# Two halves of rows in turn in the delta rule's state update, and one two-bank tile for both score maps of a head

## The chip, the cores and the metric

The kernel runs on one core of a Trainium2 chip. The metric is the device time of one execution in microseconds. The engines are named as the profile names them: PE (TensorE products; PEld its weight loads), DVE (VectorE), ACT (ScalarE), POOL, and SP, whose queue issues nearly all loads. All of them run their own instructions in order and wait for each other through semaphores.

## The reference, cut to what matters

Two layers of a block that mixes tokens in three branches, for 256 context tokens and 256 tokens of x, 1024 features, float32. The two parts that the change touches are the differential attention and the gated delta rule:

```python
def diff_softmax_combine(q, k, v, lam):                      # q, k: [b, 4 heads, 2 maps, n, 64]
    s = jnp.einsum('bhmqd,bhmkd->bhmqk', q, k) * B_HEAD_DIM ** -0.5
    p = jax.nn.softmax(s, axis=-1)
    a = p[:, :, 0] - lam * p[:, :, 1]
    return jnp.einsum('bhqk,bhkd->bhqd', a, v)

# gated delta rule, chunks of 64 tokens, forward and backward
def step(state, blk):
    u_c, w_c, qd_c, in_c, kt_c, gt_c = blk
    v_new = u_c - jnp.einsum('bhcd,bhde->bhce', w_c, state)
    o_c = jnp.einsum('bhcd,bhde->bhce', qd_c, state) + jnp.einsum('bhij,bhje->bhie', in_c, v_new)
    state = state * gt_c[..., None, None] + jnp.einsum('bhcd,bhce->bhde', kt_c, v_new)
    return state, o_c
```

Around them stand the modulation, a root-mean-square normalisation, the projections, a spatial gating branch, the gated sum of the branches and a feed-forward block with a convolution. In the second layer (the last) only the 256 tokens of x are wanted at the end.

## The kernel before, in words

**Products.** Each large product is made of float32r parts: weights come by DMA as float32 (`wr`), ACT rounds them to `wh`, DVE takes the rest `wl`, and three products per 128 rows (`mm3`) add up in a PSUM bank. The small products of attention and of the delta rule are plain float32; the trace shows each of them as two weight loads and two passes.

**PSUM.** There are eight banks of 512 float32 per partition, in four rotating groups (`BANKS`): "p" two, "g" three, "a" two, "b" one. A new tile of a group waits until an old one is released, that is, until all that reads it is done. "a" serves in turn the factor `pb` of the normalisation (`norm_end`), two column tiles of the key projections (`gdn_begin`), in layer two every second convolution tile (`gdn_conv`), the modulation products `pmod` of the mixer (`mod`), the transposed queries and keys `pqkT` (`attn_project`), and the score maps `psc` (`attn_core`).

**Order.** The framework lays out each engine's order when the kernel is built: of the instructions that its own estimate of time has as ready, the one earliest in the program goes first. Blocks in `high_priority(offset=AHEAD)` count as earlier; among them are the whole delta-rule preparation, `gdn_solve` and `gdn_scan`, between whose steps the products of `attn_project` (`ptm`), of the spatial gating (`pu`) and of `gdn_z` (`pj`) are set. In the attention the products of the branches (`pg`, `pbr`) fill in.

**Delta rule.** `gdn_scan` runs eight steps in each layer (`gdn_step`). A step works on one tile of 128 tokens: two chunks of 64, one going forward and one backward, one on partitions 0 to 63 and one on 64 to 127 (`R[0]`, `R[1]`). For the four heads it makes `pkS` (keys times state), `rhs`, `pV` (times the inverse), `vn`, where an output is wanted `pq` and `pgo`, and last `pS`, the update of the state `S` (in the trace `gS`): for each direction one bank, four products with 64 rows, then four updates on DVE. In all other products of a step the two halves alternate.

**Attention.** `attn_core` goes over tiles of 128 queries and four heads: in layer one four tiles (two with 256 keys, two with 512), in layer two two tiles with 512 keys, 24 heads in all. For each head: two score maps (`psc`, 64 rows each, map 0 on partitions 0 to 63 and map 1 on 64 to 127) in a bank of "a" each, the maximum of each on DVE, one small operation that makes the bias, two exponentials with sums on ACT, the weight `w`, the combined map, its transposition (`paT`), and the product with the values (`po`).

The steps of the change are in `bank` (line 201), `attn_core` (807 to 834) and `gdn_step` (1270 to 1280).

Of the kernel before, what the change touches and what calls it, by code (L numbers as in the profile page):

```python
# [20 lines left out]
D = 1024  # L21
# [136 lines left out]
def steps(it, *counts):  # L158
    """goes along with `it` by each of `counts` at a time."""
    for n in counts:  # L160
        for _ in range(n):
            next(it, None)
        yield
# [9 lines left out]
class _Kernel:  # L173
    def __init__(self, tc, a, out, es, dbg):
        self._gt = (None, None)
        self.tc, self.nc, self.a, self.out, self.dbg = tc, tc.nc, a, out, dbg or {}
        pool = lambda n, b, **k: es.enter_context(tc.tile_pool(name=n, bufs=b, **k))
        self.cp = pool("cp", 1)
        self.wp = pool("wp", 2)
        self.hp = pool("hp", 1)  # L180
        self.sp = pool("sp", 1)
        self.tp = pool("tp", 3)
        self.dp = pool("dp", 1, space=bass.MemoryType.DRAM)
        self.ps = pool("ps", 1, space=PSUM)
# [14 lines left out]
    BANKS = {"p": 2, "g": 3, "a": 2, "b": 1}  # L199

    def bank(self, tag, name):
        return self.ps.tile([128, 512], F32, tag=tag, name=name, bufs=self.BANKS[tag])

# [37 lines left out]
    def rsqrt(self, out, src, scale, bias, chain):  # L241
        """out = 1 / sqrt(src * scale + bias) for small tiles; bias a float, a tile of out's shape
        or, for a bare src, None."""
        nc = self.nc
        shape = list(out.shape)
        v, t = (self.cp.tile(shape, F32, tag="rsq" + n + chain, name="rsq" + n, bufs=1) for n in "vt")
        if bias is None:
            v = src
        elif isinstance(bias, float):
            self.ts(v, src, scale, bias, ALU.mult, ALU.add)  # L250
        else:
            self.stt(v, src, scale, bias, ALU.mult, ALU.add)
        self.ts(out.bitcast(I32), v.bitcast(I32), -0.5, float(0x5F3759DF), ALU.mult, ALU.add)
        self.mul(t, out, out)
        self.mul(t, t, v)
        self.stt(t, t, -10 / 3, t, ALU.add, ALU.mult)
        self.stt(out, t, 5.0, out, ALU.add, ALU.mult)
        self.mul(t, out, out)
        self.stt(t, t, -0.5 * 0.375 ** 3, v, ALU.mult, ALU.mult)
        self.stt(out, t, 1.5 * 0.375, out, ALU.add, ALU.mult)  # L260
# [10 lines left out]
    def wblock(self, src, n, step):  # L271
        """the two float32r parts of a block of weights [128, n], in pieces of `step` columns."""
        hi, lo = [], []
        r = self.wload(src, n)
        for s in range(0, n, step):
            m = min(step, n - s)
            h = self.wp.tile([128, m], F32R, tag="wh", name="wh", bufs=4)
            o = self.wp.tile([128, m], F32R, tag="wl", name="wl", bufs=4)
            self.split(h, o, r[:, s:s + m])
            hi.append(h)  # L280
            lo.append(o)
        return hi, lo
# [6 lines left out]
    def proj_fm(self, src, kt, xh, xl, c0, ps):  # L289
        """ps[:, :NT-c0] = W^T x for one column tile of W laid out [128, kt*128]."""  # L290
        wh, wl = self.wblock(src, kt * 128, 512)
        for k in range(kt):
            i, s = k // 4, slice(k % 4 * 128, k % 4 * 128 + 128)
            self.mm3(ps[:, :NT - c0], wh[i][:, s], wl[i][:, s], xh[:, k, c0:], xl[:, k, c0:], k == 0, k == kt - 1)

    def first_load(self, srcs, i, j):
        """half i of the rows of column tiles j and j + 1, to be split by first_w."""
        r = self.wp.tile([128, 2, 512], F32, tag="wr", name="wr2", bufs=3)
        for n in range(2):
            self.nc.sync.dma_start(out=r[:, n], in_=srcs[j + n][:, 4 * i:4 * i + 4].rearrange("p k m -> p (k m)"))  # L300
        self.ahead[i, j] = r
# [13 lines left out]
    def proj_first(self, srcs, xh, xl, c0, pss):  # L315
        """as proj_fm for several column tiles at once; goes along with h as its parts appear."""
# [79 lines left out]
    def load_rest(self):  # L396
        """the constants and parameters that the first products do without."""
# [33 lines left out]
    def mod_load(self, l, g, h, where):  # L431
        """half of the columns of group g, [128, 8, 256], in a slot or in tiles of a part of its size."""
        src = self.a["wmod"][l, g, h]
        if isinstance(where, int):
            r = self.slot(where, "wm", [128, 8, 256])
            self.nc.sync.dma_start(out=r, in_=src)
            return [r[:, k] for k in range(8)]
        r = []
        n = 8 // len(where)
        for i, tag in enumerate(where):  # L440
            t = self.tp.tile([128, n, 256], F32, tag=tag, name="wm2", bufs={"p4": 2, "tg": 4, "go": 4, "ta": 3}.get(tag, 1))
            self.nc.sync.dma_start(out=t, in_=src[:, n * i:n * i + n])
            r += [t[:, k] for k in range(n)]
        return r
# [4 lines left out]
    def mod_product(self, pm, r):  # L449
        """pm[32q + (ctx, x)] = silu(cond) @ w_mod over the features of k = q, q + 4."""  # L450
# [4 lines left out]
    def mod_finish(self, l, pm, j, n):  # L455
        """modv[l][:, j:j+n], features on partitions, [ctx, x]."""
# [9 lines left out]
    def mod(self, l, groups, places, tag="a"):  # L466
        """modv[l] for groups of 4 column tiles, silu(cond) @ w_mod + b_mod; yields after each half of the columns,
        which go through the next of `places` if they aren't there, and after each group."""
# [19 lines left out]
    def norm_begin(self, l, n, xf, c0, slots=(), mods=None):  # L488
        """modulate(rms_norm(x)) split into two float32r parts; x and h are feature-major. `mods` yields when the next
        half of the features has its modulation."""  # L490
# [18 lines left out]
    def norm_add(self, N, k):  # L509
        """column tile k of x: its squares, and x times its gain."""  # L510
# [11 lines left out]
    def norm_end(self, N, fill=iter(())):  # L522
        """`fill` goes along, while the tensor engine would wait."""
# [180 lines left out]
    def proj_tm(self, g, c0, use, ahead=False):  # L704
        """token-major projection onto 256 columns; use(t0, psum) for each pair of tiles of 128 tokens."""
# [22 lines left out]
    def flush(self):  # L728
        """what was put off until after the next products."""
# [77 lines left out]
    def attn_core(self):  # L807
# [5 lines left out]
        for t in range(c0 // 128, 4):  # L813
# [5 lines left out]
            for h in range(4):  # L819
# [4 lines left out]
                pss = []  # L824
                for m in range(2):
                    p = self.bank("a", "psc")
                    self.mm(p[:, :nk], self.aq[64 * m:64 * m + 64, h, 128 * t:128 * t + 128],
                            self.ak[64 * m:64 * m + 64, h, 0:nk])
                    nc.vector.tensor_reduce(out=mx[:, m:m + 1], in_=p[:, :nk], axis=AX.X, op=ALU.max)
                    pss.append(p)  # L830
                self.stt(mx, mx, -1.0, qs, ALU.mult, ALU.mult)
                for m in range(2):
                    self.act(pr[:, m, :nk], pss[m][:, :nk], AF.Exp, scale=qs[:, m:m + 1], bias=mx[:, m:m + 1],
# [37 lines left out]
    def to_tiles(self, dst, src, c0, f):  # L871
        """columns in sequence order -> columns of tiles, each two chunks: 0 and 3, then 1 and 2."""
# [14 lines left out]
    def gdn_conv(self, j, dst, cc, ssp, p=None):  # L887
        """one column tile of the projections through the convolution and silu; sums of squares per token."""
# [24 lines left out]
    def gdn_rsqrt(self, name, ssp, t0):  # L913
        """1 / length and squared length of each head of each token, [128 tokens, tile, head], from sums on 32 partitions
        per tile."""
# [42 lines left out]
    def gdn_beta(self, g):  # L958
        """beta and a projections."""
# [18 lines left out]
    def gdn_keys(self, g):  # L978
        """keys with tokens on partitions, A = strictly lower part of k k^T, decayed and scaled by beta, and the
        decay of queries and keys."""  # L980
# [63 lines left out]
    def gdn_gates(self, pbt, rk, vk):  # L1044
        """decay and write-strength columns, [128 tokens, tile, type, head]. The keys go without their 1 / length:
        with D = diag(1 / length), I + diag(beta) D M D is similar to I + diag(beta) D^2 M by D, so that beta
        takes 1 / length^2 and what goes into and comes out of the inverse the rest."""
# [98 lines left out]
    def gdn_solve(self, g):  # L1146
        """U = transpose of the inverse of I + A (forward) or inverse of I + B (backward), from 32 x 32 blocks."""
# [73 lines left out]
    def gdn_step(self, q, U, S, t, y, first, out_s, o, P):  # L1221
# [48 lines left out]
        for a in range(2):  # L1270
            d = dirs[a]
            pS = self.bank("g", "pS")
            for h in range(4):
                self.mm(pS[:, 128 * h:128 * h + 128], ktok[R[a], t, h, :], vn[R[a], 1, h, :])
            if first:
                self.act(S[:, d].rearrange("p h e -> p (h e)"), pS, AF.Copy)
            else:
                for h in range(4):
                    self.stt(S[:, d, h], S[:, d, h], q["gts"][:, a, t, 4 * y + h:4 * y + h + 1],
                             pS[:, 128 * h:128 * h + 128], ALU.mult, ALU.add)  # L1280
# [102 lines left out]
```

## Time and profile before

| | |
|---|---|
| median of 3 runs | 1662.61 us (1662.46 to 1664.08) |
| profiled execution, span of its instructions (no other time is given for it) | 1662.0 us |
| PE busy | 1623.0 us, 98% |
| DVE busy | 1084.7 us, 65% |
| ACT busy | 760.9 us, 46% |
| loads | 212 MB read, 130 GB/s over the span |

"Busy" is the time in which at least one instruction of the engine is under way. PE's instructions overlap, so a busy PE can still be slow; the distance from one pass's start to the next tells its pace. Times in the rows are microseconds from the start of the span, durations of single instructions are in ns where a row says "mean" and in us elsewhere.

### The profile page before, as it was taken

To read this page: it belongs to the slowest core of one execution; us is meant where nothing else is said; L and a number is where in the kernel's file an instruction comes from. 1 tells how busy PE (TensorE), PEld (TensorE's weight loads), DVE (VectorE), ACT (ScalarE), POOL (GpSimd) and SP (SyncE) were. 2 spreads that over 40 slices of the span, in tenths; PEclk is the share of its full clock that TensorE was granted. 3 is DMA by queue.
4 is the path that set the end of the run, shared out by engine and by line. 5 is a ranking of instruction groups with operands and counts; after the bars stand their busy time and mean duration, and the time that the engine had idled before them with its cause. 6 is when DMAs were issued, how large, how long until landed. Compare 5 with 4: busy or idle time off the path is not lost.

```text
span 1662.0 us, 28498 instructions
## 1 busy us (share of the span) xinstructions
PE 1623.0 (98%) x11278; PEld 1355.4 (82%) x11278; DVE 1084.7 (65%) x2557; ACT 760.9 (46%) x1445; POOL 6.6 (0%) x16
## 2 busy tenths in 40 slices
PE   5999999999999999999999999999999999999999
PEld 3777887876788887778888887778878799999999
DVE  5658678666744456756446655658678775788685
ACT  3553622256532333534234442653722764566564
POOL 0000000000000000000000000000000000000000
PEclk9999899999999999999999999999999999999999
DMA  8553111421233444533333335441114356755665
GB/s 327 202 192 118 40 39 52 140 89 39 74 92 102 145 147 155 213 127 93 92 107 101 97 120 169 164 154 52 40 52 140 92 153 224 226 155 174 190 185 153
DMA packets 61254, 217.24 MB, mean 131 GB/s; under 512 B 7104, under 2 KB 13248, under 8 KB 55360
## 3 DMA queue, kind: packets, MB, share of 16 engines
q1 hardware_dynamic: 59248, 207.65, 39.3%
q10 hardware_dynamic: 1872, 7.77, 1.3%
q8 instruction: 88, 1.44, 0.4%
q14 instruction: 46, 0.38, 0.1%
HBM read 212.25 MB, written 3.15 MB: 130 GB/s over the span
## 4 chain that ended last, share of the span: by engine, by line
PE 88%; DVE 5%; ACT 2%; DMA 2%; issue 1%; SPq 0%; ACTq 0%; DVEq 0%
PE pup L239 22%; PE pg L239 11%; PE pdn L239 11%; PE pqkv L239 7%; PE ptm L239 7%; PE pbr L239 6%; PE pwo L239 3%; PE pmod L239 3%; PE pu L239 2%; PE psc L239 2%; PE pS L239 2%; PE pj L239 1%; ACT U L236 1%; PE pkS L239 1%; PE po L239 1%; PE pV L239 1%
## 5 line engine op out<-in xcount | busy, mean ns | idle before, releaser
L236 ACT ACTIVATE wh<-wr 128x512 fp32r<-128x512 f32 (+1 forms) x594 | 367.6, 622 | 441.8 <-PE pdn L239 108.5
L218 DVE TENSOR_TENSOR wl<-wr,wh 128x512 fp32r<-128x512 f32 (+1 forms) x592 | 400.1, 680 | 236.1 <-ACT wh L236 233.3
L239 PE MATMUL pup<-hh,wh 128*128 128x512 f32 (+1 forms) x704 | 237.9, 338 | 1.0 <-ACT hh L236 0.9
L239 PE MATMUL pup<-hh,wl 128*128 128x512 f32 (+1 forms) x704 | 236.8, 337 | 0.0
L239 PE MATMUL pup<-hl,wh 128*128 128x512 f32 (+1 forms) x704 | 236.2, 336 | 0.0
L233 DVE SCALAR_TENSOR_TENSOR fcv<-pup,par,fcv 128x510 f32<-128x510 f32 (+1 forms) x176 | 107.3, 611 | 81.4 <-ACT fcv L236 81.1
L239 PEld LDWEIGHTS pup<-hh,wh 128*128 128x128 f32 x704 | 133.6, 190 | 17.6 <-ACT fcv L236 2.5
L239 PEld LDWEIGHTS pup<-hl,wh 128*128 128x128 f32 x704 | 133.5, 190 | 14.0 <-DVE hl L233 0.2
L239 PEld LDWEIGHTS pup<-hh,wl 128*128 128x128 f32 x704 | 133.7, 190 | 13.6
L239 PE MATMUL ptm<-wh,hh 128*128 128x256 f32 x448 | 132.1, 295 | 0.0
L239 PE MATMUL ptm<-wh,hl 128*128 128x256 f32 x448 | 131.4, 294 | 0.0
L239 PE MATMUL pg<-hh,wl 128*128 128x512 f32 (+1 forms) x384 | 130.8, 341 | 0.0
L239 PE MATMUL pg<-hh,wh 128*128 128x512 f32 (+1 forms) x384 | 130.7, 340 | 0.1
L239 PE MATMUL ptm<-wl,hh 128*128 128x256 f32 x448 | 130.6, 292 | 0.0
L239 PE MATMUL pg<-hl,wh 128*128 128x512 f32 (+1 forms) x384 | 129.9, 338 | 0.0
L239 PE MATMUL pdn<-fh,wh 128*128 128x512 f32 (+1 forms) x352 | 118.5, 337 | 0.0
L239 PE MATMUL pdn<-fh,wl 128*128 128x512 f32 (+1 forms) x352 | 118.3, 336 | 0.0
L239 PE MATMUL pdn<-fl,wh 128*128 128x512 f32 (+1 forms) x352 | 118.0, 336 | 0.0
L236 ACT ACTIVATE fcv<-pup,par 128x512 f32<-128x512 f32 (+1 forms) x88 | 51.1, 581 | 91.1 <-PE pup L239 91.1
L239 PEld LDWEIGHTS ptm<-wh,hh 128*128 128x128 f32 x448 | 88.1, 197 | 4.7 <-issue 4.2
L239 PEld LDWEIGHTS ptm<-wh,hl 128*128 128x128 f32 x448 | 88.2, 197 | 3.3 <-issue 2.9
L239 PEld LDWEIGHTS ptm<-wl,hh 128*128 128x128 f32 x448 | 87.9, 196 | 2.8 <-issue 2.2
(326 smaller groups left out, 3121.9 us busy)
## 6 DMA issues: line engine op xcount, KB each, us to landing
wr<-in_wup_dram SPq DMA_DIRECT2D x80, 512.0 KB, 3.7
wm<-in_wmod_dram SPq DMA_DIRECT2D x39, 1024.0 KB, 7.6
wr<-in_wfm_dram SPq DMA_DIRECT2D x78, 512.0 KB, 3.6
wr<-in_wtm_dram SPq DMA_DIRECT2D x32, 512.0 KB, 3.7
wr<-in_wdn_dram SPq DMA_DIRECT2D x32, 512.0 KB, 3.6
wr<-in_wbr_dram SPq DMA_DIRECT2D x24, 512.0 KB, 3.6
wr<-in_wo_dram SPq DMA_DIRECT2D x16, 512.0 KB, 4.3
wm<-in_wmod_dram SPq DMA_DIRECT2D x14, 512.0 KB, 4.2
```

The lines of the kernel that those rows point to most:

```text
L218: self.nc.vector.tensor_tensor(out=out, in0=a, in1=b, op=op)
L233: self.nc.vector.scalar_tensor_tensor(out=out, in0=a, scalar=s, in1=b, op0=op0, op1=op1)
L236: self.nc.scalar.activation(out, a, f, bias=bias, scale=scale, **k)
L239: self.nc.tensor.matmul(out, lhsT, rhs, start=start, stop=stop, **k)
```

## The change

The state update's two banks are taken together, and its products and updates go by head, the two halves of rows in turn. The score maps of a head lie in one tile of two banks, `[128, 2, 512]`, with one buffer; one reduction takes both maxima. Since group "a" is now this one tile, everything else that used it takes the halves of such a tile in turn, and a new one is made when both are given out.

```diff
-    BANKS = {"p": 2, "g": 3, "a": 2, "b": 1}
+    BANKS = {"p": 2, "g": 3, "b": 1}
 
     def bank(self, tag, name):
+        if tag == "a":
+            if not self.half:
+                pair = self.pair(name)
+                self.half = [pair[:, 1], pair[:, 0]]
+            return self.half.pop()
         return self.ps.tile([128, 512], F32, tag=tag, name=name, bufs=self.BANKS[tag])
+
+    def pair(self, name):
+
+        self.half = []
+        return self.ps.tile([128, 2, 512], F32, tag="a", name=name, bufs=1)
...
-                pss = []
+                pss = self.pair("psc")
                 for m in range(2):
-                    p = self.bank("a", "psc")
-                    self.mm(p[:, :nk], self.aq[64 * m:64 * m + 64, h, 128 * t:128 * t + 128],
+                    self.mm(pss[:, m, :nk], self.aq[64 * m:64 * m + 64, h, 128 * t:128 * t + 128],
                             self.ak[64 * m:64 * m + 64, h, 0:nk])
-                    nc.vector.tensor_reduce(out=mx[:, m:m + 1], in_=p[:, :nk], axis=AX.X, op=ALU.max)
-                    pss.append(p)
+                nc.vector.tensor_reduce(out=mx, in_=pss[:, :, :nk], axis=AX.X, op=ALU.max)
                 self.stt(mx, mx, -1.0, qs, ALU.mult, ALU.mult)
                 for m in range(2):
-                    self.act(pr[:, m, :nk], pss[m][:, :nk], AF.Exp, scale=qs[:, m:m + 1], bias=mx[:, m:m + 1],
+                    self.act(pr[:, m, :nk], pss[:, m, :nk], AF.Exp, scale=qs[:, m:m + 1], bias=mx[:, m:m + 1],
                              accum_out=sm[:, m:m + 1])
...
-        for a in range(2):
-            d = dirs[a]
-            pS = self.bank("g", "pS")
-            for h in range(4):
-                self.mm(pS[:, 128 * h:128 * h + 128], ktok[R[a], t, h, :], vn[R[a], 1, h, :])
-            if first:
-                self.act(S[:, d].rearrange("p h e -> p (h e)"), pS, AF.Copy)
-            else:
-                for h in range(4):
-                    self.stt(S[:, d, h], S[:, d, h], q["gts"][:, a, t, 4 * y + h:4 * y + h + 1],
-                             pS[:, 128 * h:128 * h + 128], ALU.mult, ALU.add)
+        pSs = [self.bank("g", "pS") for _ in range(2)]
+        for h in range(4):
+            for a in range(2):
+                self.mm(pSs[a][:, 128 * h:128 * h + 128], ktok[R[a], t, h, :], vn[R[a], 1, h, :])
+        if first:
+            for a in range(2):
+                self.act(S[:, dirs[a]].rearrange("p h e -> p (h e)"), pSs[a], AF.Copy)
+            return
+        for h in range(4):
+            for a in range(2):
+                self.stt(S[:, dirs[a], h], S[:, dirs[a], h], q["gts"][:, a, t, 4 * y + h:4 * y + h + 1],
+                         pSs[a][:, 128 * h:128 * h + 128], ALU.mult, ALU.add)
```

## Rows read from the trace of the kernel before

**Rows 1.** The page: busy time by engine, and the chain that ended last.
```profile
PE 1623.0 (98%) x11278; PEld 1355.4 (82%) x11278; DVE 1084.7 (65%) x2557; ACT 760.9 (46%) x1445; POOL 6.6 (0%) x16
...
PE 88%; DVE 5%; ACT 2%; DMA 2%; issue 1%; SPq 0%; ACTq 0%; DVEq 0%
```
**Rows 2.** Busy times by stretch (us, instructions), clock, DMA: scan and attention, each layer.
```profile
205.00:304.00 99.00, 99.00 (x936) 77.84 (x933) 75.70 (x248) 23.30 (x39) 0.00 (x0) 1.00 0.16 49
341.00:440.00 99.00, 97.41 (x454) 67.25 (x453) 66.21 (x213) 62.08 (x164) 0.00 (x0) 1.00 0.20 59
1201.00:1272.00 71.00, 70.11 (x649) 53.94 (x648) 54.93 (x167) 16.05 (x27) 0.00 (x0) 1.00 0.23 68
1300.00:1340.00 40.00, 38.90 (x227) 27.95 (x227) 28.57 (x82) 27.82 (x72) 0.00 (x0) 1.00 0.27 80
```
**Rows 3.** The chain in order of time (start, us, piece), in the second scan.
```profile
1247.75 1.64 PE pS L239 x16
```
**Rows 4.** Groups by shape on PE: count, busy us, mean ns, idle before.
```profile
L239 PE MATMUL psc<-akT,qhT 64*128 64x512 f32 x64 | 28.5, 641 | 0.2 <-ACT pr L236 0.2
L239 PE MATMUL pS<-vn,ktok 64*128 64x128 f32 x256 | 27.4, 285 | 0.6 <-DVE vn L218 0.6
L239 PE MATMUL psc<-akT,qhT 64*128 64x256 f32 x32 | 8.9, 428 | 0.0
```
**Rows 5.** Time line of PE (start, us to the last end, instruction): one step.
```profile
233.82 1.09 PE L239 MATMUL pgo<-vn,inT 64*64 64x128 f32 x16
234.84 1.71 PE L239 MATMUL pS<-vn,ktok 64*128 64x128 f32 x16
236.48 0.38 PE L239 MATMUL ptm<-wh,hl 128*128 128x256 f32 x1
```
**Rows 6.** Time line of weight loads in that step, two short windows.
```profile
235.17 0.30 PEld L239 LDWEIGHTS pS<-vn,ktok 64*128 64x128 f32 x2
...
235.40 0.41 PEld L239 LDWEIGHTS pS<-vn,ktok 64*128 64x128 f32 x6
```
**Rows 7.** Time line of DVE, the same step's updates of the state.
```profile
236.30 2.15 DVE L233 SCALAR_TENSOR_TENSOR gS<-gS,g_gts,pS 128x128 f32<-128x128 f32 x8
```
**Rows 8.** Time line of PE: score products of four heads.
```profile
367.26 0.70 PE L239 MATMUL psc<-akT,qhT 64*128 64x256 f32 x4
...
371.67 0.70 PE L239 MATMUL psc<-akT,qhT 64*128 64x256 f32 x2
...
410.81 1.12 PE L239 MATMUL psc<-akT,qhT 64*128 64x512 f32 x2
...
1309.08 1.55 PE L239 MATMUL psc<-akT,qhT 64*128 64x512 f32 x4
```
**Rows 9.** Groups by shape from 300 to 1340: maxima on DVE, exponentials on ACT.
```profile
L829 DVE TENSOR_REDUCE mx<-psc 128x1 f32<-128x512 f32 x32 | 21.8, 686 | 5.1 <-PE psc L239 4.7
L829 DVE TENSOR_REDUCE mx<-psc 128x1 f32<-128x256 f32 x16 | 6.5, 419 | 3.4 <-PE psc L239 2.9
...
L236 ACT ACTIVATE pr<-psc,mx,qscale 128x512 f32<-128x512 f32 x32 | 24.6, 774 | 2.6 <-DVE mx L233 2.5
L236 ACT ACTIVATION_READ_ACCUMULATOR pr<-psc,mx,qscale 128x1 f32 x47 | 9.3, 199 | 0.0
```
**Rows 10.** Waits (us in total, times, longest), 341 to 440 and 1300 to 1340.
```profile
PEld psc L239 <- ACT pr L236: 2.3, 9, 0.4
...
PEld psc L239 <- ACT pr L236: 0.9, 2, 0.5
```
**Rows 11.** Time line of DVE, normalisation at the start of layer two.
```profile
1042.03 1.69 DVE L233 SCALAR_TENSOR_TENSOR hl<-xn,modv,hh 128x256 fp32r<-128x256 f32 x4
...
1049.36 1.28 DVE L218 TENSOR_TENSOR xn<-xn,pb 128x512 f32<-128x512 f32 x2
```
**Rows 12.** The chain in order of time, the key projections of layer two.
```profile
1042.45 22.22 PE pqkv L239 x96
```
**Rows 13.** Time line of PE, modulation products in layer one.
```profile
81.99 2.78 PE L239 MATMUL pmod<-wm,scond 128*32 128x256 f32 x42
```

More of the change, by code (lines that the diff above doesn't have):

```diff
@@ L174, in __init__ @@
     def __init__(self, tc, a, out, es, dbg):
-        self._gt = (None, None)
+        self._gt, self.half = (None, None), []
         self.tc, self.nc, self.a, self.out, self.dbg = tc, tc.nc, a, out, dbg or {}
```

## The prediction, before the changed kernel was run

> **What bounds the kernel now.** I read the page first. PE is busy 98% of the span, and the chain of work that ended last is 88% PE [rows 1]; the other engines are busy two thirds of the time or less. So an edit is worth what it takes out of PE's own stream, as long as other work stands ready for PE in that stage. That is the next thing to look for, in the busy times by stage [rows 2]: in both delta-rule scans (205 to 304 and 1201 to 1272) and both attention stages (341 to 440 and 1300 to 1340) PE is busy 97% or more, while DVE has 67 to 77% and ACT 23 to 70%. The reader should see that no second engine is near its limit there, and that PE is fed by other products between the steps. The chain of waits agrees: fifteen of the sixteen state updates of the scans stand on it as whole pieces of 1.6 to 1.7 us, of which one row is shown [rows 3]. The two things that the change touches are therefore on the path: the state update's products (pS) keep PE 27.4 us in all, the score products (psc) 28.5 + 8.9 = 37.4 us [rows 4]. "Busy" is not speed, though; the last thing to read is at what pace these passes go, and that is where both edits act.
>
> **The change, part by part.**
>
> *1. State update, products.* A step has 8 products, each of two passes, 16 in all. Half of them use array rows 0 to 63, half rows 64 to 127. Now all 8 passes of the first half go ahead of the second. The time line of one step shows pS starting at 234.84 and the next product at 236.48, so 1.64 us; just ahead of it pgo, with the same 16 passes and operands of the same length but its two halves in turn, takes 1.02 us to pS's start [rows 5]. The weight loads of pS show why. Early in the step two loads take 0.30 us: one load lasts 0.19, so they start 0.11 apart, one after the other. In the middle, where the first half's end meets the second half's beginning, six loads take 0.41 us: 0.22 for five starts [rows 6]. There the two halves run side by side, two passes per 0.11 us. With the halves in turn the whole step should run like its middle: 8 pairs at 0.11 us plus one pass of 0.285 [rows 4] is 1.17 us in place of 1.71 [rows 5], 0.54 less. Sixteen steps: 8.6 us. The best end is pgo's own length, 1.09: 0.62 x 16 = 9.9 us. The worst end is no gain, if the full-width loads can't keep up over a whole step (a rival below). I take 8.5 us, since the nearest row is this very tile's middle.
>
> [...]
>
> *2. State update, on DVE.* The 8 updates of a step take 2.15 us, 0.27 each [rows 7], and keep their number and size. The next step's first product needs head 0 in both directions: now after the 5th update, then after the 2nd, 0.8 us sooner; its last product needs the 8th either way. PE has ptm and pu products to do meanwhile [rows 2], so I cost this at nothing. Both PSUM banks must be free before the first pair, where now the second is needed half a step later; its former reader (tq or vn) is over before pgo starts in most steps, so nothing again. If that cover is gone, either is worth at most 0.8 us in 14 steps, 11 us, to one side or the other.
>
> *3. Scores, products.* A head's two maps are two products of two passes, again on the two row halves. The rows show them in three states [rows 8]: of 256 columns, four passes issued together take 0.70 us, as long as two alone (0.70); of 512 columns, one map alone takes 1.12 us, and two issued near each other 1.55. Now the second map has its own bank and its own wait, so that many heads come in two pieces or half overlapped. With one tile both wait for the same thing and start together: 16 heads x 1.12 + 8 heads x 0.70 = 23.5 us in place of 37.4 [rows 4]. That is 13.9 us less at best.
>
> *4. Scores, the wait.* What pays for it: the tile has one buffer, so the first product of the next head waits until both exponentials have read it. Now it waits for one. The second exponential and its sum take 0.774 + 0.199 = 0.97 us [rows 9]. PE runs in order; behind the waiting product stand paT and po of the head before, and the filling products of the branches; who waits for those is ACT and DVE with the weights' splits. Nothing to the full 0.97 us in 24 heads (23.3 us) can become idle PE. Today PE's wait for that release is 2.3 + 0.9 us over the two stages [rows 10], with other products laid in between, and more of them are to be had in both stages. I take 0.3 us a head, 7 us, nearer to the row than to the bound. So parts 3 and 4 together: 7 us less; ends 13.9 less and 9.4 more.
>
> *5. Scores, the maximum.* Two reductions become one. From 419 ns at 256 columns and 686 at 512 [rows 9], 267 ns per 256 columns, one of 1024 should take 1.22 us and one of 512 0.69: DVE loses 0.15 us x 24 = 3.7 us of work, where it is not the bound [rows 2]. But the step from the second product's end to the exponentials grows by 0.53 us (512 columns). The attention stages have the later branch's products to fill PE, so nothing; uncovered it would be 0.53 x 16 = 8.6 us.
>
> *6. The same two banks elsewhere.* All users of tag "a" (modulation products, the normalisation's pb, key projections, pqkT) now get halves of one tile, and a new pair must wait for both halves of the old one. In the second layer the key projections 2 and 3 wait for pb, which is read until 1050.64, while products run from 1042.45 [rows 11, 12]. Today three of four column tiles can go with the features as they appear; then two, 6 products per feature tile at 22.22 / 96 = 0.23 us, 1.4 us, against 1.28 / 2 + 1.69 / 2 = 1.49 us of DVE per feature tile. So PE is a little short: about 0.1 us x 6, plus a start, 1 us. In the first layer the modulation products that fill a hole at 82 to 88 (42 of them in 2.78 us) [rows 13] belong to two groups; the second must then wait until the first has been read, and 32 products, 2.1 us, go to another place, where PE may have a hole too. I take 2 us for the whole part; the ends are 0 and 8, for the later convolutions of layer two, which take halves in turn.
>
> **Sum.** -8.5 - 7 + 2 = -13.5 us on the profiled execution's span of 1662.0 gives 1648.5. The median of the runs is 1662.61, 0.6 above that span, so I predict 1649 us. Its own range, from the sizes of parts 1, 4 and 6, is 1643 to 1655.
>
> **The rivals.**
>
> A. *The scores give nothing back.* PE starts the pair together but stands for it as long as it saves, because the order of PE's instructions is laid out at build and the exponentials come later than it assumes. For it: in the second layer's attention heads follow each other by the chain product, maximum, exponential. Against: small waits today [rows 10]. -8.5 + 2 gives 1656.
>
> B. *Weight loads take turns.* Part 1 gives nothing, the scores as forecast: -7 + 2, 1657.6. For it: two single loads are 0.11 us apart. Against: the middle of the step [rows 6]. [...]
>
> C. *Slower: the pair's release starves PE.* Place: the 24 heads. Price: 0.97 us of wait and up to 0.53 us of longer maximum, 1.5 us a head, 36 us if all of it lies open, against 13.9 + 8.5 us saved and 2 us lost at the other users of the banks. It decides when more than 20.4 / 36 = 57% is open; at 80% it is 28.8 - 20.4 = +8.4, 1671 us. For it: one buffer where there were two, and an engine that runs in order. Against: both stages have products of three branches to put between.
>
> D. *All of it pays.* -9.9 - 13.9, nothing lost: 1639 us.
>
> E. *It does not do what it says*: neither pair overlaps further, since what sets the pace is issue, not rows: 1662 us.
>
> **How the numbers follow.** Forecast 0.50, A 0.18, B 0.06, C 0.12, D 0.07, E 0.07. What a measurement of this kernel can tell from no change is about 0.2%, 3.3 us: faster means under 1659.3. The forecast, D, A and most of B are faster: 0.78. E and the edges of A and B are the same: 0.11. C is slower: 0.11. The range that leaves out no more than 2 in 10 takes in D, the forecast, A and B: 1639 to 1662.
>
> **What would show it.** Part 1: pS from its start to the next product at 1.1 us a step in place of 1.64, and 18 to 19 us in all in place of 27.4; at 1.6 B is right. Part 3: psc at 1.12 and 0.70 us a head, 24 us in all. Part 4: PE's wait for the release by the exponentials; above 20 us, C. Part 6: PE idle or slow near 85 and between 1042 and 1054. If PE's busy groups shrink as said and the span does not, the prediction is wrong in its premise that PE sets the time of these stages.

## The result, and the profile after

The changed kernel takes 1688.45 us (median of 4 runs, 1685.03 to 1689.43), the kernel before beside it 1663.34 (1662.46 to 1665.03): a ratio of 1.0138, 95% interval 1.0126 to 1.0150, so 23 us slower where 14 us faster was predicted. (The two medians lie 25.1 us apart, just outside that interval; the text goes by the ratios.) All ratios here and below are of fast executions; one of e12's ten (3121.33 us) was slow and counts in its median alone. The profiled execution took 1689.18 us, its span 1687.4.

The page of the changed kernel: busy time of PE, the clock that PE was granted in 40 slices, and the chain that ended last.
```profile
PE 1630.1 (97%) x11278; PEld 1352.2 (80%) x11278; DVE 1086.3 (64%) x2533; ACT 766.5 (45%) x1449; POOL 6.6 (0%) x16
...
PEclk9989999999999999999999999899999999999999
...
PE 82%; DVE 8%; ACT 5%; issue 2%; DMA 1%; SPq 0%; ACTq 0%; DVEq 0%
```
Against [rows 1] the reader sees the same 11278 PE instructions, 7 us more busy time, and a chain that is PE for 82% in place of 88%, with 6 more points for DVE and ACT together (13 for 7). Nothing in these lines says where. Three places do.

**What the change was meant to do, it did.** The time line of PE, one step of the changed kernel's first scan (start, us to the last end, instruction), answers [rows 5]; the next two fences are the weight loads of one step [rows 6], of the kernel before (the step of [rows 5]) and of the changed one, the last fence its score products [rows 8].
```profile
220.75 0.93 PE L249 MATMUL pgo<-vn,inT 64*64 64x128 f32 x14
221.61 1.16 PE L249 MATMUL pS<-vn,ktok 64*128 64x128 f32 x16
222.70 0.39 PE L249 MATMUL ptm<-wh,hh 128*128 128x256 f32 x1
```
```profile
234.84 1.52 PEld L239 LDWEIGHTS pS<-vn,ktok 64*128 64x128 f32 x16 [0.17 <-issue]
```
```profile
221.61 0.97 PEld L249 LDWEIGHTS pS<-vn,ktok 64*128 64x128 f32 x16 [0.17 <-issue]
```
```profile
381.62 0.70 PE L249 MATMUL psc<-akT,qhT 64*128 64x256 f32 x4
...
434.32 1.13 PE L249 MATMUL psc<-akT,qhT 64*128 64x512 f32 x4
```
pS runs 1.09 us from its start to the next product where it took 1.64, a head of scores 1.13 or 0.70. The groups by shape say the same in sums (count, busy us, mean ns, idle before and its releaser), answering [rows 4]; pkS, the next step's first products, is with them, in the first fence for the changed kernel, in the second for the kernel before.
```profile
L249 PE MATMUL pkS<-gS,kT 128*64 128x128 f32 x224 | 31.8, 296 | 1.4 <-DVE gS L243 0.9
L249 PE MATMUL psc<-akT,qhT 64*128 64x512 f32 x64 | 21.7, 649 | 3.2 <-ACT pr L246 3.1
L249 PE MATMUL pS<-vn,ktok 64*128 64x128 f32 x256 | 19.1, 285 | 0.0
...
L249 PE MATMUL psc<-akT,qhT 64*128 64x256 f32 x32 | 6.3, 428 | 0.0
```
```profile
L239 PE MATMUL pkS<-gS,kT 128*64 128x128 f32 x224 | 23.5, 290 | 0.1
```
pS fell from 27.4 to 19.1 us, psc from 37.4 to 28.0. But pkS, untouched by the diff, rose from 23.5 to 31.8: as much as pS saved.

**The scans did not become shorter.** Busy times by stretch, from the first pV to the last pS of each scan: kernel before, then changed kernel.
```profile
209.10:303.50 94.40, 94.40 (x871) 73.90 (x870) 72.52 (x239) 20.67 (x36) 0.00 (x0) 1.00 0.17 51
1198.70:1271.50 72.80, 71.91 (x671) 55.57 (x670) 55.62 (x167) 18.33 (x32) 0.00 (x0) 1.00 0.22 66
```
```profile
217.80:318.30 100.50, 99.76 (x893) 73.95 (x892) 73.65 (x242) 23.06 (x37) 0.00 (x0) 1.00 0.17 48
1220.10:1298.10 78.00, 76.67 (x711) 57.67 (x709) 57.32 (x169) 20.38 (x36) 0.00 (x0) 1.00 0.25 75
```
6.1 and 5.2 us longer. Of this, 22 and 40 more passes of other products, at 0.12 us from one to the next (ptm at 226.39, 226.51, 226.63 in the changed kernel), are 2.6 and 4.8 us, and pS by the time lines takes 4.0 and 4.6 us less; so some 7.5 and 5 us are passes that have become slower, for PE is busy nearly throughout.

**The starts of both layers became longer.** The same view for the first products of a layer (keys, queries, values): before, then after.
```profile
60.00:116.50 56.50, 55.87 (x349) 41.57 (x347) 30.43 (x62) 34.00 (x67) 0.00 (x0) 1.00 0.58 205
1042.40:1104.00 61.60, 61.55 (x357) 49.82 (x358) 39.40 (x77) 39.89 (x82) 0.00 (x0) 1.00 0.40 124
```
```profile
60.00:125.00 65.00, 59.84 (x326) 44.42 (x324) 31.40 (x64) 34.98 (x68) 0.00 (x0) 0.92 0.42 144
1055.00:1126.00 71.00, 66.44 (x360) 52.64 (x360) 38.45 (x76) 39.83 (x82) 0.00 (x0) 0.93 0.36 108
```
The first stretch ends with the products of beta (pba) that follow these, the second begins and ends with these products, to within 0.7 us. They are 8.5 and 9.4 us longer; PE stands idle 5.2 and 4.6 us in them, and its mean granted clock is 0.92 and 0.93 in place of 1.00. The time line of PE shows where the two come from (in brackets the idle time before, and what ended it; ssp and psq make the lengths of the delta rule's queries and keys). The kernel before comes first, then the changed one.
```profile
84.69 1.05 PE L239 MATMUL psq<-cst,sse 128*128 128x4 f32 x8
85.68 0.64 PE L239 MATMUL pmod<-wm,scond 128*32 128x256 f32 x8
86.14 0.62 PE L239 MATMUL ssp<-csq,cst 128*32 128x128 f32 x16
86.57 1.04 PE L239 MATMUL pmod<-wm,scond 128*32 128x256 f32 x14
```
```profile
84.85 1.93 PE L249 MATMUL pqkv<-wm,scond 128*32 128x256 f32 x32
90.26 1.87 PE L249 MATMUL psq<-cst,sse 128*128 128x4 f32 x8 [3.48 <-ACT sse L246]
92.39 1.08 PE L249 MATMUL ssp<-csq,cst 128*32 128x128 f32 x16 [0.27 <-DVE rkv L931]
94.62 0.76 PE L249 MATMUL pqkv<-hh,wh 128*128 128x512 f32 x1 [1.15 <-DVE rk L243]
...
1085.88 0.65 PE L249 MATMUL ssp<-csq,cst 128*32 128x128 f32 x8 [2.27 <-ACT csq L246]
1088.12 0.77 PE L249 MATMUL pqkv<-hh,wh 128*128 128x512 f32 x1 [1.58 <-DVE cv L243]
```
(Halves of a pair bear the name of the pair's first user, so modulation products read pqkv here.) In the kernel before, psq started at 84.69 with no wait, between modulation products that filled the hole (42 passes before it [rows 13], 8 and 14 behind). Now 32 of these 64 passes stand there, the other half are elsewhere, and PE waits 3.48 us. The stretches around these waits, with the clock in the eighth place:
```profile
89.20:99.30 10.10, 7.63 (x35) 6.11 (x36) 4.26 (x14) 6.39 (x11) 0.00 (x0) 0.50 0.36 146
99.30:110.00 10.70, 10.70 (x54) 8.41 (x54) 4.08 (x7) 4.82 (x9) 0.00 (x0) 1.00 0.16 49
1076.00:1085.80 9.80, 7.62 (x57) 5.99 (x55) 5.37 (x8) 7.73 (x17) 0.00 (x0) 1.00 0.36 107
1085.80:1092.60 6.80, 5.13 (x19) 3.78 (x20) 1.50 (x2) 1.96 (x5) 0.00 (x0) 0.50 0.30 80
```
The granted clock is 0.50 over a stretch of 10.1 us that begins in the wait of 3.48 us and holds the two after it, and over one of 6.8 us that begins as the wait of 2.27 us ends and holds that of 1.58. PE is busy for 7.6 and 5.1 us of them; one 512-column pass then follows another after 0.43 us (95.18, 95.61, 96.04), not after 0.23 as at a granted clock of 1.00 (100.33, 100.56, 100.79). So time is lost twice in these places, once as idle time and once as slow work. An estimate from these rows: 4.5 us more idle time and 3.8 us of slow work (half of 7.6) make nearly all of the first 8.5 us; 4.5 and 2.6 are most of the second 9.4, and 3.5 us at 0.52 from 1055.1 on add some 1.7.

### The profile page after: what moved, and what is told of

It is laid out like the page before. It is cut to its first block, busy times and chain, and to the rows that moved or that the text cites. A ratio compares the mean times of both kernels' runs of the same rounds, so it can differ in the third digit from the quotient of the medians.

```text
span 1687.4 us, 28497 instructions
## 1 busy us (share of the span) xinstructions
PE 1630.1 (97%) x11278; PEld 1352.2 (80%) x11278; DVE 1086.3 (64%) x2533; ACT 766.5 (45%) x1449; POOL 6.6 (0%) x16
## 4 chain that ended last, share of the span: by engine, by line
PE 82%; DVE 8%; ACT 5%; issue 2%; DMA 1%; SPq 0%; ACTq 0%; DVEq 0%
PE pup L249 22%; PE pdn L249 11%; PE pg L249 11%; PE pqkv L249 7%; PE ptm L249 7%; PE pbr L249 5%; PE pwo L249 3%; PE pu L249 2%; PE pmod L249 2%; PE pj L249 2%; PE pkS L249 2%; DVE wl L228 1%; ACT U L246 1%; PE pV L249 1%; PE pE L249 1%
```

## The experiments

All ran beside the kernel before. "Difference" is (ratio - 1) x 1663.4 us; the kernel before had medians of 1663.3 to 1665.5 us in the four groups of runs, so it can lie a few us from the difference of two medians. Layers are counted from here on as layer 0 and layer 1, the first and the second. A "piece" of pkS is a run of its passes on PE with no other product between.

| kernel | us | ratio, 95% interval | difference |
|---|---|---|---|
| the change | 1688.45 | 1.0138 [1.0126, 1.0150] | +23.0 |
| e1 state update alone | 1672.36 | 1.0054 [1.0036, 1.0071] | +9.0 |
| e2 pair and shared halves alone | 1675.23 | 1.0068 [1.0051, 1.0085] | +11.3 |
| e3 update's products alone | 1663.46 | 0.9995 [0.9985, 1.0005] | -0.8 |
| e4 pair alone, nothing shared | 1655.99 | 0.9951 [0.9937, 0.9966] | -8.2 |
| e5 = e3 + e4 | 1655.15 | 0.9941 [0.9922, 0.9960] | -9.8 |
| e6 = e1 + e4 | 1667.93 | 1.0025 [1.0013, 1.0036] | +4.2 |
| e7 = e2, layers' starts unshared | 1660.15 | 0.9979 [0.9968, 0.9990] | -3.5 |
| e8 update's order on DVE alone | 1674.94 | 1.0061 [1.0039, 1.0083] | +10.1 |
| e9 = e8, turns of two heads | 1671.68 | 1.0037 [1.0026, 1.0048] | +6.2 |
| e10 = e8, pkS from the last head | 1661.28 | 0.9968 [0.9956, 0.9980] | -5.3 |
| e11 = e5, pkS from the last head | 1642.45 | 0.9857 [0.9842, 0.9872] | -23.8 |
| e12 = e5, projection z later | 1668.59 | 1.0012 [0.9996, 1.0027] | +2.0 |

**e1 and e2: the change in two.** e1 has the new `gdn_step` and the old score code and banks; e2 the rest of the diff, with the old `gdn_step`.

> The kernel before with the state update alone in its new order (products and updates by head, halves in turn); group "a" and the scores as before. Theory S (the changed kernel's loss comes from the shared two-bank tile at the other users of group "a"): 1657 to 1667 us, no loss at the start of either layer; in the scans pS falls by 4 us a layer and pkS grows by about 3, as in the changed kernel. Rival U (the loss comes from the updates' order, which cuts pkS into pieces): 1672 us or more. Rival W (the scores' common wait): about 1654, the forecast gain of part 1.

> The changed kernel with the state update in its old order; the pair tile for scores and halves of it for all other users of group "a" stay. Theory S: 1678 to 1686 us, with PE idle near 90 and 1086 and the clock down there, as in the changed kernel. Rival U: 1660 to 1666. Rival W: 1680 or more, but with the loss in the attention stages.

e1 came out as rival U had it, with pS down by 8.8 us in all and pkS up by 7.9. e2's 1675.23 lies between the ranges of theory S and U and fits none of the three. Both halves cost, 9.0 and 11.3 us; their sum, 20.3, is near the 23.0 of the whole, so most of the loss isn't made by the two meeting. Each had to be taken apart further.

**e3: the products in turn, the updates as before.**
```
-            pS = self.bank("g", "pS")
-            for h in range(4):
-                self.mm(pS[:, 128 * h:128 * h + 128], ktok[R[a], t, h, :], vn[R[a], 1, h, :])
+        pSs = [self.bank("g", "pS") for _ in range(2)]
+        for h in range(4):
+            for a in range(2):
+                self.mm(pSs[a][:, 128 * h:128 * h + 128], ktok[R[a], t, h, :], vn[R[a], 1, h, :])
```


> The kernel before with only the products of the state update in turn; the eight updates on DVE go one half after the other as before. If what pS saves was given back by pkS because of the order of the updates: pS 9 us in each scan in place of 13.5, pkS about 10 as before, 1654 to 1657 us. If the scans are not set by PE: 1661 to 1664 with the same pS.

No difference, though the products are as fast as in the changed kernel and pkS is back at 23.6 us. The time is that of the second value expected; its reason, that PE doesn't set the scans, is not what the trace shows. Layer 0 keeps some of the saving: from its first pV to that of layer 1 it takes 987.1 us, before 989.6. In layer 1 the saving is there at first: from the first pV to the first pj it takes 82.3 us (1196.7 to 1279.0), before 87.1 (1198.7 to 1285.8). From there to the last of the branches' pg it takes 156.3 us where it took 148.5. What stands between is the start of the attention; e3's time line there, and its busy times around it:
```profile
1296.13 1.12 PE L239 MATMUL psc<-akT,qhT 64*128 64x512 f32 x2
1299.81 1.12 PE L239 MATMUL psc<-akT,qhT 64*128 64x512 f32 x2 [2.55 <-ACT pr L236]
1301.32 1.11 PE L843 MATMUL paT<-cst,pr 128*128 128x128 f32 x4 [0.40 <-DVE pr L233]
1302.37 2.07 PE L239 MATMUL psc<-akT,qhT 64*128 64x512 f32 x2
```
```profile
1296.00:1320.00 24.00, 20.93 (x98) 14.03 (x97) 15.09 (x41) 16.95 (x43) 0.00 (x0) 0.86 0.18 55
```
Two heads' scores follow each other with no product of a branch between, PE waits 2.55 us for the exponential, and behind it psc takes 2.07 us at 1302.37 for 1.12, with a mean granted clock of 0.86 over these 24 us. 3 us idle and 24 x 0.14 = 3.4 us of clock are most of the 7.8 lost. In the kernel before, 20 passes of pg stand at 1301.09 between those heads, and the next scores wait 0.21 us:
```profile
1303.95 1.88 PE L239 MATMUL psc<-akT,qhT 64*128 64x512 f32 x4 [0.21 <-ACT pr L236]
```
Such a wait before psc, of 1.59 to 2.65 us, is in every kernel here that has the products in turn, but for e11: in e1, e5, e6, e12 and the change (2.64 us at 1327.41).

**e4: the pair of banks in the attention alone.** A PSUM pool for these two banks is closed and opened anew around `attn_core`; all other users get two single banks as before.
```
+        self.a_pool("pair")
         yb = self.attn_core()
+        self.a_pool("a")
...
+                pss = self.pair("psc")
...
+                nc.vector.tensor_reduce(out=mx, in_=pss[:, :, :nk], axis=AX.X, op=ALU.max)
```


> The kernel before with the score pair and the one reduction, but the pair has a pool of its own that takes the place of group "a" only while attention runs; all other users keep two separate banks; state update as before. Theory S: the start of both layers and the feed-forward as before, attention of layer one about 5 us shorter: 1655 to 1659 us. Rival W (the common wait costs what the pairs save or more): 1662 or more.

8.2 us faster. The pair itself pays; what turns it into e2's loss is only that other stages get their banks as halves of it: 11.3 + 8.2 = 19.5 us.

**e7: where the sharing costs.** As e2, but with two single banks from a layer's normalisation to its last key, query and value product; from the attention's projections on, halves.
```
+        self.a_pool("pair")
         self.attn_project()
...
+            if last:
+                self.a_pool("a")
             early = self.mod(1, (4, 5, 6), (5,), "g") if last else iter(())
```


> The pair of score banks with the old state update; the halves of a pair are shared by other users of these banks from the attention's projections on to the next layer's start, and only in the first products of each layer (pb, the keys' pqkv, modulation) stand two single banks again. Theory, the sharing costs at the layers' starts (pqkv end +8.6 us in layer 0, +9.3 us in layer 1 after the change): 1675.2 - 18 = 1656 to 1660. Rival, the sharing costs along the attention's projections and the FFN as well: 1665 to 1675.

1660.15, just past the end of what the theory gave: 14.8 of the 19.5 us lie at the starts, 4.7 elsewhere. PE has no idle time beyond that of before in the stretches at the starts any more, and the first has its clock back. The second, with a clock of 0.97, is 2.4 us longer than before; but so it is in e4 (64.0 us, 0.97), where nothing is shared:
```profile
60.00:116.00 56.00, 55.37 (x347) 41.23 (x345) 29.95 (x61) 33.91 (x67) 0.00 (x0) 1.00 0.57 205
1040.00:1104.00 64.00, 64.00 (x362) 51.27 (x363) 39.76 (x77) 40.69 (x84) 0.00 (x0) 0.97 0.38 120
```
Of the 4.7 us some 3 lie in layer 0's feed-forward block: from its first pup to its last pdn (their starts) it takes 371.7 us in e7 and 368.6 in e4, with a wait of 1.7 us before pup that e4 hasn't. What makes that wait was not tested.

**e5 and e6: the parts put together without the sharing.** e5 is e3's and e4's edit, e6 e1's and e4's.

> Kernel before with the sixteen update products of a step issued with their halves of rows in turn (updates on VectorE one half after the other, as before) and with the pair of score banks taken in the attention alone. Alone, the first edit gave 1663.46 (no change) and the second 1655.99 (-8). Theory 1, the saving of the products is real but lost where nothing of the attention can take it: the two add up, 1655 to 1657. Theory 2, the saving was given back at the first scores of layer 1's attention (PE idle 2.55 us at 1299.81 before psc), a place that the pair changes: then some of it comes through, 1648 to 1653. Theory 3, both use the same slack: over 1658.

> The whole change without the sharing of halves: new order of products and of updates, and the pair with its one reduction, in banks that only the attention uses so. If the order of the updates costs its 9 us wherever the scores stand (theory 1): 1663 to 1666, no change against before. If its loss was made in layer 1's attention (idle 1.59 us at 1305.69 before psc, and the clock after it), which the pair changes (theory 2): 1655 to 1658. Against the changed kernel's 1688.45 either value puts 22 to 33 us on the sharing.

e5's theory 1 holds: -0.8 and -8.2 add up to -9.0, measured -9.8, and the wait at the attention's start is still there (2.64 us before psc at 1292.12). e6 is 4.2 us slower than before, above both values expected, nearer to theory 1. The order of the updates, e6 against e5, costs 14.0 us; the sharing, the change against e6, 18.8.

**e8 and e9: VectorE's order alone.** The products stay one half after the other; the eight updates go in turn by one head (e8) or by two (e9).
```
+            for h in range(4):
+                for a in range(2):
+                    self.stt(S[:, dirs[a], h], S[:, dirs[a], h], q["gts"][:, a, t, 4 * y + h:4 * y + h + 1],
+                             pSs[a][:, 128 * h:128 * h + 128], ALU.mult, ALU.add)
```
```
+            for h, a in ((0, 0), (1, 0), (0, 1), (1, 1), (2, 0), (3, 0), (2, 1), (3, 1)):
```


> Kernel before with VectorE's eight updates of a step in turn over the halves; the products stay one half after the other. Theory 1, the order of the updates by itself costs the 9 us of e1 (the next step's first products are cut up and wait for VectorE): 1669 to 1675. Theory 2, the cost comes only of both orders together: 1662 to 1665. What layer to look at: the spans of pV (209.1 to 298.6 and 1198.7 to 1266.7 before).

> Kernel before with VectorE's eight updates of a step in the order heads 0, 1 of one half, heads 0, 1 of the other, then heads 2, 3 likewise: half as fine a turn as in e8 (1674.94). Theory 1, what costs is that the first products of the next step (pkS) stand in more pieces among full-tile passes: the two scans hold 44 pieces of pkS before, 62 in e8, and 56 here, so two thirds of e8's 11.5 us: 1669 to 1673. Theory 2, the cost is that the first half's state is complete later (update 7 instead of 4 of 8; here update 6): 1669 to 1675 too; this run alone doesn't part them, e10 does.

10.1 and 6.2 us slower, both within what their first theories gave (e9's second theory had the same range; e10 parts the two). The order of eight instructions on an engine that is busy three quarters of the time costs more than all that the products' order could save. All of e8's loss lies in its two scans, which are 6.0 and 4.2 us longer than before. The second (busy times by stretch) has one PE pass more than before, the same work, and 4.2 us more of PE's busy time:
```profile
1203.70:1280.70 77.00, 76.11 (x672) 57.01 (x670) 55.63 (x167) 18.37 (x32) 0.00 (x0) 1.00 0.21 62
```
The time line of one of its steps shows what makes the passes slower.
```profile
1248.34 0.43 PE L239 MATMUL pkS<-gS,kT 128*64 128x128 f32 x2
1248.71 0.39 PE L239 MATMUL pu<-hl,wh 128*128 128x256 f32 x1
1249.02 0.43 PE L239 MATMUL pkS<-gS,kT 128*64 128x128 f32 x2
1249.39 0.39 PE L239 MATMUL pu<-hh,wh 128*128 128x256 f32 x1
1249.61 0.28 PE L239 MATMUL pu<-hh,wl 128*128 128x256 f32 x1
1249.73 0.27 PE L239 MATMUL pu<-hl,wh 128*128 128x256 f32 x1
```
With the halves in turn, each pair of updates sets one head of the next step's pkS free, two updates or 0.54 us after the last by [rows 7]. PE's order was laid out with a full-width pass or three in each such gap, so pkS stands in pieces. PE hardly waits there: before pkS it is idle 0.2 us in all in e8, 0.1 before. A pass of pu that follows another starts 0.12 us after it (1249.61, 1249.73); alone between two pieces it takes 0.31 (1248.71 to 1249.02). A piece of two pkS passes takes 0.36 to 0.37, one of four no more (1246.86 to 1247.23). Counted in the time lines of both scans, pkS stands in 44 pieces before, 62 in e8, 56 in e9, and 70 in the changed kernel. These rows account for most of the loss: from each piece's start to the next product pkS takes 20.5 us before and 25.0 in e8, and a run of full-width passes between pieces takes 0.2 us more than 0.12 a pass, which is 3.5 us for 18 runs; together 8 of the 10.1 us.

**e10 and e11: fewer pieces.** pkS goes through the heads from the last to the first, so that its first pair needs the last update; e10 has e8's updates, e11 is e5 with this line.
```
-            for h in range(4):
+            for h in reversed(range(4)):
                 for a in range(2):
                     self.mm(pk[R[a], 128 * h:128 * h + 128], q["kT"][:, h, 128 * t + 64 * a:128 * t + 64 * a + 64], S[:, dirs[a], h, :])
```


> e8's order of updates, but the next step's first products (pkS) go through the heads from the last to the first. Their first pair then needs the last update, so the eight start later and stand in 19 pieces in the two scans instead of 62 (44 before). Theory 1, the pieces cost (about 0.24 us for each more run of products on PE, from e1 and e8): the loss of 11.5 us goes and some more with it, 1650 to 1660. Theory 2, what costs is that a step begins later after its updates: three more updates to wait for in 28 steps, 1675 to 1690.

> e5 (products in turn, updates one half after the other, pair in banks of its own; 1655.15) with pkS through the heads from the last to the first: 22 pieces of pkS in the two scans instead of 44. By theory 1 (pieces cost) 22 pieces and as many runs between them fewer, at 0.24 us some 8 to 10 us: 1643 to 1650, unless layer 1's attention gives it back as it did with the products' saving (then 1650 to 1653). By theory 2 (a later start costs): over 1658.

e10 is faster than before, with the very order of updates that cost 10.1 us, and 15.4 us better than e8: the pieces cost, not the order of the updates nor the later start (of which there are 14, not the 28 of the expectation). Of the 19 pieces left, nine are a step's whole sixteen passes in 1.02 us, as in e10's time line here, and the other five steps stand in 14 and 2:
```profile
1225.32 1.09 PE L239 MATMUL pkS<-gS,kT 128*64 128x128 f32 x16
1226.34 0.39 PE L239 MATMUL pu<-hh,wl 128*128 128x256 f32 x1
```
The median, 1661.28, lies just past the weak end of what was expected (1650 to 1660): layer 1's attention gave back some of the gain, with 1.59 us idle before psc at 1293.31 and the clock at 0.86 in this stretch of e10:
```profile
1291.00:1316.00 25.00, 21.75 (x108) 14.59 (x107) 17.47 (x46) 17.00 (x46) 0.00 (x0) 0.86 0.23 66
```
e11 is the best kernel of the study, 1642.45 us, 23.8 under before and 14.0 under e5, just past the good end of what theory 1 gave. Beside 22 pieces fewer, its first scores in layer 1 happen to have other products between them, and the clock stays whole in the stretch that answers to the last one:
```profile
1281.00:1320.00 39.00, 36.25 (x239) 27.08 (x238) 31.62 (x80) 29.10 (x74) 0.00 (x0) 1.00 0.29 87
```
From the first pj to the last pg it takes 147.4 us there, in e5 151.5: so some 4 of the 14 us are this, the rest lies earlier.

**e12: a cover that was put in the wrong place.** z's projection of layer 1 is issued behind the attention's code.
```
-        z = self.gdn_z()
-        if l > 0:
+        if l == 0:
+            z = self.gdn_z()
+        else:
             self.lam(l)
...
+        if l > 0:
+            z = self.gdn_z()
         yacc = self.branch(0, self.parts(ya, "ya", 4, 5), None, False)
```


> e5 with the projection z (pj, 96 passes, 12 us) of layer 1 issued behind the attention instead of ahead of it, so that its passes can stand between the first scores and their products. Theory, the products' saving was given back where layer 1's attention begins with nothing else for PE (idle 2.64 us at 1292.12 before psc in e5, granted clock 0.86 over the next 25 us): idle and clock loss go, 5 to 6 us come through, 1648 to 1651. Rival, the attention's chain sets its length whatever PE has beside it: 1654 to 1656.

Both expectations were wrong: 11.8 us worse than e5. z's passes were laid out early all the same (the first pj at 1273.1, as in e5), with the attention's first heads among them, and the later heads were left with nothing beside them. Busy times by stretch of e12:
```profile
1300.00:1340.00 40.00, 28.01 (x159) 20.48 (x158) 24.39 (x70) 23.59 (x61) 0.00 (x0) 0.87 0.21 66
```
The time line of PE has idle stretches of 0.7 to 2.4 us in head after head from 1305 to 1331. That PE without cover loses time in the attention is shown by it, but not that cover at the first heads would have brought the products' saving through.

## Why the prediction was wrong, by its own steps

Three terms of the sum failed. The sharing of the banks (part 6) was put at a loss of 2 us and cost 19.5; the order of the updates (part 2) was put at nothing and cost 10.1; the products (part 1) shrank as forecast, but of the 8.5 us they were to give only 0.8 came through.

**Part 1, the products: size right, worth wrong.** 8.5 us were forecast; pS fell by 8.3 [rows 4 and the groups after]. Rival B, that loads take turns, is out: 16 loads took 0.97 us, one per 61 ns, where one half after the other they took 1.52. The 0.11 us between two loads [rows 6], which spoke for that rival, is between loads on one half; with the two halves in turn the loads are not that far apart. But by e3 the saving alone is worth 0.8 us, with zero inside the interval. The step that failed is the premise that PE's time is everywhere as good as any other: what layer 1 had saved by its first pj, 4.8 us, its attention lost to a wait and to the clock, 7.8 us. This is read from the time line of e3; no run took that wait away and left all else.

**Part 2, the updates on DVE: costed at nothing, measured 10.1 us** (e8; e1 against e3 9.8, e6 against e5 14.0). I reasoned that pkS's first head comes free sooner and its last no later, and that PE has other products meanwhile. Both are so, and that is the fault: the other products (seen in [rows 5]; [rows 2], which I named for them, doesn't show them) go between the heads, and each such change of shape cost PE time both ways: in e8 a full-width pass that takes 0.12 us among its like took 0.31 between two pieces, and a piece of two pkS passes 0.36, nearly as long as one of four (0.37). Why a change costs time was not shown. The 11 us that I gave as the end, "at most 0.8 us in 14 steps" to either side, came near in size by chance, for the mechanism was another.

**Parts 3 and 4, the scores: the sum right, in part by luck.** -7 forecast, -8.2 measured where nothing is shared (e4). Both terms were too large and made up for each other: the products save 9.4 us (28.0 left, not the 23.5 of every head overlapped) where I set 13.9, and PE's idle time before psc, nearly all of it for the exponentials, grew from 0.2 us to 3.2, in e4 to 0.8, where I set 7. The 3.2 us of today from which I had set it [rows 10] are waits of the weight loads; PE itself stood idle 0.2 us [rows 4]. A wait above 20 us would have meant rival C. So C, the one rival that ended slower, named the wrong place.

**Part 5, one maximum: right in size.** The groups of DVE after (count, busy us, mean ns), answering [rows 9]:
```profile
L838 DVE TENSOR_REDUCE mx<-psc 128x2 f32<-128x1024 f32 x16 | 19.5, 1220 | 2.9 <-PE psc L249 2.9
```
1.22 us, as worked out. e4 shows that it does not outweigh the pair's gain.

**Part 6, the shared banks: 2 us forecast, ends 0 and 8, measured 19.5** (e2 against e4; 18.8 from the change against e6). This is the largest error. Of its two holes the one near 85 was the right place, and the mechanism there, modulation products that must go elsewhere, is what the time line shows: 32 passes, the number that I gave, are gone from there. The second came at 1083 to 1088, not at the start of the key projections (1042 before, 1055 now). There PE's last wait before the next products of the pair is for the convolution (cv), which fits one half of a pair still being read while PE wants the next pair; that reason is read from the row and not tested by itself. I had put that at the far end of 8 us and priced only waits. The rows show two things that I did not price: waits of 2.3 to 3.5 us at once, and stretches of 10.1 and 6.8 us at a granted clock of 0.50 with them. At the starts that makes 8.5 + 9.4 us by the stretches, 14.8 by e7.

**The sum.** By experiments: products -0.8, updates +10.1, scores -8.2, sharing +19.5, together +20.6; measured +23.0. The 2.4 us left over are not assigned; the intervals of the kernels that the terms come from reach 1.7 (e3) to 3.7 us (e8) to each side.

That the whole gain of -13.5 was expected on PE's side, and its busy groups pS and psc did shrink by 17.7 us while the time grew, is what the prediction named as the sign that its premise is wrong.

What stays open: why the first heads' scores of layer 1 are laid out with or without other products between them. Where the wait is (e1, e3, e5, e6, e10, the change), all 96 passes of pu already stand between the first pV and the last pS of that layer's scan; before and in e8, which haven't the wait, 75. But e11 has all 96 there too, and no wait before psc. No run was aimed at it but e12, which missed. Open too is what the sharing costs outside the layers' starts.

## What to carry to other kernels

Where PE is the bound and alternates between products on parts of its array and full-width ones, count the pieces, not only the passes: a piece more cost about half a microsecond here (10.1 us for 18 in e8, 6.2 for 12 in e9), and the order of another engine's instructions decides how many there are, so let a group of small products wait for the last of its inputs and run whole. Before the users of two buffers are given halves of one, ask at each of them what PE will do while the slower half is read, and price such a wait with the slow work that came with it here (10.1 and 6.8 us at a granted clock of 0.50).

## What the runs showed of the hardware that was not expected

- Sixteen weight loads of 64 rows by 128 columns, in turn on the two row halves, took 0.97 us, while their matmuls run; one half after the other they took 1.52 us in the kernel before.
- A full-width pass of 256 columns starts 0.12 us after its like, but a single one between two pieces of half-width products holds PE 0.31 us; two passes of pkS in a piece take 0.36 us, four 0.37, sixteen 1.02.
- The granted clock was 0.50 over 10.1 us that begin in a wait of PE of 3.48 us and hold waits of 0.27 and 1.15, and over 6.8 us that begin as a wait of 2.27 us ends and hold one of 1.58; in e3, behind a wait of 2.55 us before psc, two passes of psc took 2.07 us for 1.12, and the mean granted clock of the 24 us around was 0.86.
